# Low parts of weights by adding transfers, and GpSimd's work in another order, in a one-layer decoder step

## The chip, the cores and the metric

The kernel runs on one core of a Trainium2 chip. The metric is the device time of one execution in microseconds. A core has five engines that run beside each other and meet by semaphores: TensorE (PE in the profile, its weight loads PEld), VectorE (DVE), ScalarE (ACT), GpSimd (POOL) and SyncE (SP), which here issues most of the transfers. Each engine takes its instructions in the order in which they were put in its queue.

## What is computed

One inference step of one layer of width 2048, for 256 new tokens of a prompt and 8 x 4 tokens of running sequences (288 columns in all). Cut to what matters:

```python
h = rmsnorm(x, norm1_g)
proj = h @ w_in + b_in                      # 2048 -> 3072
a, gate, z = split(proj, 1024)
u = a * sigmoid(gate)
u_ext = concat([hist_conv, u])              # 30 older rows
c = silu(layernorm(depthwise_causal_conv(u_ext, conv_w, 31 taps) + conv_b))
z_ext = concat([hist_pool, z])              # 15 older rows
d = mean over windows (2, 4, 8, 16) of z_ext, by group of 256 columns, minus z
p = (d @ pool_w, by group) * pool_scale
x = x + concat([c, p]) @ w_out              # 2048 -> 2048
h2 = rmsnorm(x, norm2_g)
x = x + square(relu(h2 @ w_ff1)) @ w_ff2    # 2048 -> 8192 -> 2048
y = rmsnorm(x, norm_f)                      # also returned: the new u and z history
```

## The kernel before

All data lies with channels on the 128 partitions and the 288 tokens along the free dimension. To keep float32 precision, each product of a weight tile and an activation tile is done in three matmuls: high weight by high activation, low weight by high activation, high weight by low activation. For that every weight is split on the chip into a high part (`whi`, rounded by ScalarE) and a low part (`wlo`, the rest).

A weight block is loaded by SyncE in two halves of 512 KB (`load`, line 164), each into one of six raw buffers `wr`. `split` (line 276) makes the two parts of each half, each into one of five buffers, so a high part can be written only when TensorE is done with the part five before. How the low part comes about is set by a letter in `WAYS` (line 73), one for each half in turn:

- V: VectorE subtracts, one instruction of 128 x 1024 (line 265);
- G: GpSimd subtracts, two instructions of 128 x 512 (line 268);
- D: ScalarE writes the negated high part (line 262), and a transfer issued by GpSimd adds the weights to it from memory (line 263). D needs the raw buffer only for the high part.

`SEQUENCE` (line 45) gives the first stages: eight conv blocks c0 to c7, four pool groups p3 to p0 and their small products P3 to P0. A conv block or a pool group is 96 matmuls, and takes two weight blocks, that is four parts; a small product is 12 matmuls and one part of half length. Then follow w_out on the pool half (the projection, weights w0 to w7), w_out on the conv half, and the two feed-forward products in four chunks. In `gemm` (line 296) the matmuls of two k and one output bank come in sixes: two with whi, two with wlo, two with whi. The weights of a stage are split while the stage before is multiplied.

A conv block's result goes through VectorE and ScalarE (`conv_pair`, line 427), then through 31 taps on VectorE (lines 446 to 448); for the running sequences GpSimd multiplies all windows by the taps (`prd`, line 451) and VectorE sums them (line 453). The taps are emitted under `later()`, with a low urgency. The sums of the conv blocks feed a mean (`ln_mean`) inside the sixth product of the projection. A pool group (`pool_group`, line 464) goes through doubling sums on GpSimd (line 479), three small GpSimd operations (lines 483, 486, 487) with a VectorE subtraction between them (line 484), and a split into `dx`; `pool_products` (line 495) multiplies it.

The order of each queue is set when the program is built: a scheduler that simulates the engines picks by urgency and by what is ready in its simulation. `tc.issue_after(x)` puts an instruction behind x in the order of issue. `classes` (line 317) reorders the next matmuls of a `gemm` by the parity of the activation row that they read; `TURN` (line 70) is such an order and stands in c2, c5, the projection's first product, its products g = 5 and g = 7, in g = 2 of the conv half, and in the feed-forward's second product. `between` places other work inside a `gemm`, ahead of the pair (k, bank) named as its key.

Of the kernel before, what the change touches and what calls it, by code (L numbers as in the profile page):

```python
# [12 lines left out]
ALU = mybir.AluOpType  # L13
# [56 lines left out]
TURN = "110100" * 4 + "01" * 6 + "1100" * 3  # L70


WAYS = {"c2": "GVGV", "c3": "GDGG", "c4": "GDGD", "p3": "GDDG", "c5": "GDGD", "c": "GGGV", "p": "GVVG", "w0": "VV", "w": "GG", "ff": "VV"}


VEC = (("norm1_g", 16), ("b_in", 24), ("conv_b", 8), ("ln_g", 8), ("ln_b", 8), ("pool_scale", 8), ("norm2_g", 16), ("norm_f", 16))
# [10 lines left out]
def trunk_kernel(ctx: ExitStack, tc: tile.TileContext, io):  # L87
# [18 lines left out]
    def nm(s):  # L106
        seen[s] = seen.get(s, 0) + 1
        return f"{s}{seen[s]}"
# [25 lines left out]
    def f32(t):  # L134
        return t.bitcast(F32)
# [25 lines left out]

    blocks = iter(range(5, io["w"].shape[0]))

    def load():

        src, raw = io["w"][next(blocks)], []
        for h in range(2):
            raw.append((raw_tile(), src[:, 4 * h : 4 * h + 4, :]))
            nc.sync.dma_start(*raw[-1])
        return raw  # L170
# [81 lines left out]
    turns = {}  # L252

    def split_part(raw, src, hi, lo, way):

        nc.scalar.copy(hi, raw)  # L260
        if way == "D":
            nc.scalar.activation(lo, f32(hi), AF.Copy, scale=-1.0)
            nc.gpsimd.dma_start(lo, src, accum_op=ALU.add)
        elif way == "V":
            nc.vector.tensor_tensor(lo, raw, f32(hi), op=ALU.subtract)  # L265
        else:
            for j in range(0, raw.shape[1], 2):
                nc.gpsimd.tensor_tensor(lo[:, j : j + 2, :], raw[:, j : j + 2, :], f32(hi[:, j : j + 2, :]), op=ALU.subtract)  # L268
# [7 lines left out]
    def split(halves, stage="ff"):  # L276

        parts = []
        for raw, src in halves:
            turns[stage] = turns.get(stage, -1) + 1  # L280
            parts.append(spl())
            ways = WAYS.get(stage) or WAYS[stage[0]]
            split_part(raw, src, *parts[-1], ways[turns[stage] % len(ways)])
        return lambda k, m: columns(*parts[k // 4], k % 4, m)
# [8 lines left out]
            chain[0] = last.ins  # L293
        return last

    def gemm(banks, rhs, m_outer=False, between={}, classes="", by_part=False, gets=None, pairs=None):


        n = len(rhs)
        gets = gets or ready.pop(0)  # L300
        todo, begins = [], {}
        if by_part:
            for k in range(0, n, 2):
                sets = [range(len(banks))] if k else [range(2), range(2, len(banks))]
                for last, ms_ in enumerate(sets, 1 - len(sets)):
                    for part, (w, x) in enumerate(((0, 0), (1, 0), (0, 1))):
                        if last == 0:
                            begins[len(todo)] = (k, None, k + 1)[part]
                        todo += [(k + (1 - d if x else d), m, w, x) for m in ms_ for d in range(2)]
        else:  # L310
            pairs = pairs or [(k, m) for k in range(0, n, 2) for m in range(len(banks))]
            if m_outer:
                pairs.sort(key=lambda km: km[1])
            for k, m in pairs:
                begins[len(todo)] = (k, m) if m else k
                todo += [(k + d, m, w, x) for d, w, x in ((0, 0, 0), (1, 0, 0), (0, 1, 0), (1, 1, 0), (1, 0, 1), (0, 0, 1))]
        head = todo[: len(classes)]
        for j, c in enumerate(classes):
            todo[j] = next(p for p in head if c == "." or (p[0] + p[3]) % 2 == int(c))
            head.remove(todo[j])  # L320
# [91 lines left out]
    rb = row("rb")  # L412


    cs, pcs = [], []
    sum_c = tmpp.tile([P, 2, T], F32, name="sum_c", tag="ag2", bufs=2)

    def history(i):
# [8 lines left out]
    def conv_pair(i, banks):  # L427
# [8 lines left out]
            nc.vector.scalar_tensor_tensor(out=out, in0=a, scalar=v("b_in", i), in1=b, op0=ALU.add, op1=ALU.mult)  # L436
        if i % 2 == 0:
            cs.append(actp.tile([P, 2, T], F32, name=nm("c"), tag="c", bufs=4))
        c = cs[i // 2][:, i % 2, :]
        with later():  # L440
            if i % 2 == 0:
                pcs.append(cvp.tile([P, 2, SEQ], F32, name=nm("pc"), tag="cv"))
            pc = pcs[i // 2][:, i % 2, :]
            cwv = vec[:, CWO + i * CW : CWO + (i + 1) * CW]
            nc.scalar.activation(pc, up[:, 0:SEQ], AF.Identity, bias=v("conv_b", i), scale=cwv[:, 0:1])  # L445
            for w in range(1, CW):
                dst = pc if w < CW - 1 else c[:, 0:SEQ]
# [3 lines left out]
            nc.gpsimd.tensor_tensor(prd[:, :, :, 0:CW], windows(us, CW), cwv[:, None, None, :].to_broadcast([P, NB, NS, CW]), op=ALU.mult)  # L451
# [12 lines left out]
    def pool_group(g):  # L464
# [19 lines left out]
        nc.vector.scalar_tensor_tensor(out=d[:, :, 0:SEQ], in0=s[:, :, PH:ZO], scalar=1.0 / w, in1=z[:, :, PH:ZO], op0=ALU.mult, op1=ALU.subtract)  # L484
        news = [x[:, :, ZO:ZL].rearrange("p m (b t) -> p m b t", t=ZS)[:, :, :, PH:] for x in (s, z)]
        nc.gpsimd.tensor_scalar(news[0], news[0], 1.0 / w, None, op0=ALU.mult)
        nc.gpsimd.tensor_tensor(d[:, :, SEQ:T].rearrange("p m (b t) -> p m b t", t=NS), news[0], news[1], op=ALU.subtract)
        dh, dl = act2("dx", tag="p", bufs=4)
        nc.scalar.copy(dh, d)
        nc.vector.tensor_tensor(dl, d, f32(dh), op=ALU.subtract)  # L490
# [34 lines left out]
    for kind, i in SEQUENCE[3:-1]:  # L525
        if (kind, i) == ("P", 1):
            continue
        if kind == "c":
            conv_pair(i, conv_products(i, classes=TURN if i == 5 else "", **(dict(gets=ahead(1), between={12: lambda: pool_products(1)}) if i == 7 else {})))
# [9 lines left out]
    gemm(each(bks[0]) + each(bks[1]), proj, gets=[lambda k, m: both_gets[m // 2][0](k, m % 2)], between={(0, 2): lambda: pool_products(0)}, classes="." * 36 + TURN, pairs=early + [(6, m) for m in range(4)])  # L539
    chain.clear()  # L540
    load_table(AF.Abs_reciprocal_sqrt, f32(mixp[1][0])[:, 0:1])
    with later(2 * LATER):
# [53 lines left out]
    chain.append(last)  # L596
    bks = [bank2() for _ in range(2)]
    two_gets = [ahead(0) for _ in range(2)]
    gemm(each(bks[0]) + each(bks[1]), mixc, gets=[lambda k, m: two_gets[m // 2][0](k, m % 2)])
    chain.clear()  # L600
    for g in range(8):
        bk = bks[g] if g < 2 else bank2()
# [179 lines left out]
```

## Time and profile before

| | us |
|---|---|
| median of three runs | 1082.34 (1081.94 to 1082.63) |
| the profiled execution | 1082.43 |
| its span, first to last instruction | 1080.6 |

The page's first part gives each engine's busy time; its fourth the chain of work that ended last. In the timeline a row is: start, duration, engine, line, operation, output<-inputs, shape, count, and in brackets the idle time before it with what ended it. In the windows view a row is a stretch of time, its length, then busy time and number of instructions of PE, PEld, DVE, ACT and POOL, the granted TensorE clock, the busy share of the transfer engines and GB/s. The waits view reads: engine, what it was about to write, its line, what it waited for, total us, times, longest.

### The profile page before, as it was taken

What the parts mean: (1) busy time and instruction counts of PE and PEld (TensorE: products, weight loads), DVE (VectorE), ACT (ScalarE), POOL (GpSimd) and SP (SyncE); (2) the same over time, 40 slices, a digit from 0 to 9 for tenths busy, and PEclk for the clock granted to TensorE, in tenths of its full rate; (3) what the DMA queues carried; (4) which work ended last, traced back from release to release, by engine and by line L of the source; (5) the groups of instructions that cost most, each with busy time, mean ns of one, the idle gap of its engine ahead of it and who ended that gap; (6) DMA issues with size and microseconds to landing.
All of it is one profiled execution on the core that took longest, in us unless ns stands there. A gap on an engine that the chain in (4) does not pass through costs nothing.

```text
span 1080.6 us, 19528 instructions
## 1 busy us (share of the span) xinstructions
PE 1069.2 (99%) x8176; PEld 1067.9 (99%) x8176; DVE 633.7 (59%) x810; ACT 479.0 (44%) x588; POOL 175.9 (16%) x182
## 2 busy tenths in 40 slices
PE   9999999999999999999999999999999999999996
PEld 8999999999999999999999999999999999999996
DVE  7899999788654544444554444555544445554553
ACT  8654445665544433334443333444433334444441
POOL 0878979512000000000000000000000000000001
PEclk9999999999999999999999999999999999999999
DMA  9896478555555555555555555555555555555522
GB/s 326 288 263 182 145 187 247 177 171 173 162 173 166 169 175 163 170 173 165 170 174 164 170 170 167 171 173 162 173 168 167 173 171 164 173 166 170 172 79 88
DMA packets 58296, 190.71 MB, mean 176 GB/s; under 512 B 6240, under 2 KB 11232, under 8 KB 58208
## 3 DMA queue, kind: packets, MB, share of 16 engines
q1 hardware_dynamic: 56336, 184.35, 54.3%
q0 software_dynamic: 1008, 3.67, 1.9%
q8 instruction: 64, 1.05, 0.4%
q10 hardware_dynamic: 864, 1.44, 0.4%
q14 instruction: 24, 0.20, 0.0%
HBM read 185.16 MB, written 4.28 MB: 175 GB/s over the span
## 4 chain that ended last, share of the span: by engine, by line
PE 75%; issue 21%; ACT 2%; POOL 1%; DMA 1%; SPq 0%; POOLq 0%; DVE 0%
PE ac L291 74%; POOL wlo L268 1%; DMA wr<-in_w 1%; ACT whi L349 1%; PE pp L291 1%; DMA wlo<-in_w 1%; ACT hx L354 0%; ACT z_all L405 0%; POOL prd L451 0%; POOL xT L718 0%; ACT whi L260 0%; SPq L191 0%; POOLq L768 0%; DVE xT L691 0%; ACT whi L356 0%
## 5 line engine op out<-in xcount | busy, mean ns | idle before, releaser
L260 ACT CAST whi<-wr 128x1024 fp32r<-128x1024 f32 (+1 forms) x332 | 346.5, 1044 | 551.3 <-PE ac L291 536.7
L265 DVE TENSOR_TENSOR wlo<-wr,whi 128x1024 fp32r<-128x1024 f32 x288 | 353.5, 1227 | 348.1 <-ACT whi L260 348.1
L291 PE MATMUL ac<-ax,whi 128*128 128x288 f32 x2048 | 351.0, 292 | 0.0
L291 PE MATMUL ac<-fx,whi 128*128 128x288 f32 x2048 | 350.2, 292 | 0.0
L291 PEld LDWEIGHTS ac<-ax,whi 128*128 128x128 f32 x2048 | 296.0, 187 | 0.0
L291 PEld LDWEIGHTS ac<-fx,whi 128*128 128x128 f32 x2048 | 295.6, 187 | 0.0
L291 PE MATMUL ac<-ax,wlo 128*128 128x288 f32 x1024 | 217.3, 292 | 0.0
L291 PE MATMUL ac<-fx,wlo 128*128 128x288 f32 x1024 | 216.4, 292 | 0.0
L291 PEld LDWEIGHTS ac<-ax,wlo 128*128 128x128 f32 x1024 | 162.5, 187 | 0.0
L291 PEld LDWEIGHTS ac<-fx,wlo 128*128 128x128 f32 x1024 | 162.2, 187 | 0.0
L291 PE MATMUL ac<-hx,whi 128*128 128x288 f32 x768 | 131.9, 296 | 1.4 <-DVE hx L352 1.4
L718 POOL TENSOR_TENSOR xT<-xT,rf 128x288 f32<-128x288 f32 x4 | 3.1, 795 | 799.9 <-ACT rf L722 799.9
L291 PEld LDWEIGHTS ac<-hx,whi 128*128 128x128 f32 x768 | 112.6, 190 | 1.8 <-ACT hx L354 1.7
L268 POOL TENSOR_TENSOR wlo<-wr,whi 128x512 fp32r<-128x512 f32 x74 | 102.4, 1433 | 17.1 <-ACT whi L260 16.0
L448 DVE SCALAR_TENSOR_TENSOR pc<-u_all,vec,pc 128x256 f32<-128x256 f32 x232 | 99.3, 479 | 1.9 <-ACT pc L445 0.7
L291 PE MATMUL ac<-hx,wlo 128*128 128x288 f32 x384 | 80.4, 295 | 0.2 <-DMA wlo<-in_w 0.2
L291 PEld LDWEIGHTS ac<-hx,wlo 128*128 128x128 f32 x384 | 61.1, 189 | 0.4 <-DMA wlo<-in_w 0.4
L291 PE MATMUL ac<-dx,whi 128*128 128x288 f32 x256 | 46.8, 295 | 0.0
L291 PE MATMUL ac<-mx,whi 128*128 128x288 f32 x256 | 44.9, 293 | 0.0
L660 DVE SCALAR_TENSOR_TENSOR t<-ac,r 128x576 f32<-128x576 f32 x32 | 24.2, 757 | 25.4 <-PE ac L291 25.3
L291 PEld LDWEIGHTS ac<-dx,whi 128*128 128x128 f32 x256 | 38.4, 188 | 0.2
L291 PEld LDWEIGHTS ac<-mx,whi 128*128 128x128 f32 x256 | 37.5, 188 | 0.2 <-DVE xT L579 0.2
(129 smaller groups left out, 529.6 us busy)
## 6 DMA issues: line engine op xcount, KB each, us to landing
wr<-in_w SPq DMA_DIRECT2D x335, 512.0 KB, 3.8
wlo<-in_w POOLq DMA_DIRECT2D x7, 512.0 KB, 7.8
xT<-in_xT SPq DMA_DIRECT2D x8, 288.0 KB, 7.7
wr<-in_w SPq DMA_DIRECT2D x5, 256.0 KB, 3.9
out_u_out<-u_all SPq DMA_DIRECT2D x1, 1208.0 KB, 9.6
u_all<-in_hist_c SPq DMA_DIRECT2D x8, 136.0 KB, 5.3
out_z_out<-z_all SPq DMA_DIRECT2D x1, 668.0 KB, 9.2
z_all<-in_hist_p SPq DMA_DIRECT2D x4, 152.0 KB, 6.6
```

What stands on the lines that cost most here:

```text
L260: nc.scalar.copy(hi, raw)
L265: nc.vector.tensor_tensor(lo, raw, f32(hi), op=ALU.subtract)
L268: nc.gpsimd.tensor_tensor(lo[:, j : j + 2, :], raw[:, j : j + 2, :], f32(hi[:, j : j + 2, :]), op=ALU.subtract)
L291: last = nc.tensor.matmul(*args, **kw)
L349: nc.scalar.copy(hi[:, blocks[0]], raw[:, blocks[0]])
L448: nc.vector.scalar_tensor_tensor(out=dst, in0=up[:, w : w + SEQ], scalar=cwv[:, w : w + 1], in1=pc, op0=ALU.mult, op1=ALU.add)
L660: nc.vector.scalar_tensor_tensor(out=t, in0=bk[:, :, :T], scalar=0.0, in1=both(rows2[0]), op0=ALU.max, op1=ALU.mult)
L718: eng.tensor_tensor(xk, xk, r[:, None, :].to_broadcast([P, n, T]), op=ALU.mult)
```

## The change

- `WAYS`: the second low part of each of p2, p1, p0 and the third (V) become D, and the second of c6 and of c7 (G) become D: eight in all. The second of c4 goes from D to G, the first of w0 from V to G. There were seven D parts, there are fourteen.
- `prd` of conv blocks 0 and 1 is issued behind the first adding transfer, that of block 2 behind the second, those of all later blocks behind the third. The taps of blocks 2 and 3 are emitted one block later.
- GpSimd's weight subtractions of c7 and w0 are issued behind p1's last GpSimd operation, those from w1 on behind p0's. In a pool group VectorE's subtraction now stands behind the three small GpSimd operations.
- P1's products stand 24 matmuls earlier in c7 (k = 8 instead of 12), P0's 12 matmuls earlier in the projection.
- The halves of w0 to w7 are loaded in the other order, the half used first being loaded first. The first 24 matmuls of the projection take all high weights before the low ones (`late`).
- The first product of the conv half takes, for its first four k, two banks to the end before the other two (`mixed`).

```diff
-WAYS = {"c2": "GVGV", "c3": "GDGG", "c4": "GDGD", "p3": "GDDG", "c5": "GDGD", "c": "GGGV", "p": "GVVG", "w0": "VV", "w": "GG", "ff": "VV"}
+WAYS = {"c2": "GVGV", "c3": "GDGG", "c4": "GGGD", "p3": "GDDG", "c5": "GDGD", "c": "GDGV", "p": "GDDG", "w0": "GV", "w": "GG", "ff": "VV"}
...
-    def load():
+    def load(order=(0, 1)):
...
-        for h in range(2):
+        for h in order:
...
-            nc.gpsimd.dma_start(lo, src, accum_op=ALU.add)
+            added.append(nc.gpsimd.dma_start(lo, src, accum_op=ALU.add))
...
-                nc.gpsimd.tensor_tensor(lo[:, j : j + 2, :], ...)
+                with tc.issue_after(pooled[-1].ins) if pooled else nullcontext():
+                    nc.gpsimd.tensor_tensor(lo[:, j : j + 2, :], ...)
...
+        todo[:late] = sorted(todo[:late], key=lambda p: p[2])
...
-            get = split(load(), f"w{j}")
-            yield [lambda k, m, get=get: get(korder[k], m)]
+            get = split(load((1, 0)), f"w{j}")
+            yield [lambda k, m, get=get: get(korder[k] ^ 4, m)]
...
+        while waiting:
+            taps(*waiting.pop())
+        if i in (2, 3):
+            waiting.append((i, up, us))
+        else:
+            taps(i, up, us)
+
+    def taps(i, up, us):
...
-            nc.gpsimd.tensor_tensor(prd[:, :, :, 0:CW], ...)
+            with tc.issue_after(added[max(0, min(2, i - 1))].ins):
+                nc.gpsimd.tensor_tensor(prd[:, :, :, 0:CW], ...)
...
-        nc.vector.scalar_tensor_tensor(out=d[:, :, 0:SEQ], ...)
...
-        nc.gpsimd.tensor_tensor(d[:, :, SEQ:T]..., news[0], news[1], op=ALU.subtract)
+        last = nc.gpsimd.tensor_tensor(d[:, :, SEQ:T]..., news[0], news[1], op=ALU.subtract)
+        newest[g] = last
+        nc.vector.scalar_tensor_tensor(out=d[:, :, 0:SEQ], ...)
...
+        if i == 7:
+            pooled.append(newest[1])
...
-... between={12: lambda: pool_products(1)} ...
+... between={8: lambda: pool_products(1)} ...
...
+    pooled.append(newest[0])
...
+    mixed = [(k, m) for k in range(0, KT // 2, 2) for m in range(4)]
+    mixed.sort(key=lambda km: (km[0] // 4, km[1] // 2) if km[0] < 4 else (1, 0))
-    gemm(..., between={(0, 2): lambda: pool_products(0)}, classes="." * 36 + TURN, ...)
+    gemm(..., late=24, between={4: lambda: pool_products(0)}, classes="." * 24 + TURN, ...)
...
-    gemm(each(bks[0]) + each(bks[1]), mixc, gets=[...])
+    gemm(each(bks[0]) + each(bks[1]), mixc, gets=[...], pairs=mixed)
```

More of the change, by code (lines that the diff above doesn't have):

```diff
@@ L70 @@
 TURN = "110100" * 4 + "01" * 6 + "1100" * 3
-WAYS = {"c2": "GVGV", "c3": "GDGG", "c4": "GDGD", "p3": "GDDG", "c5": "GDGD", "c": "GGGV", "p": "GVVG", "w0": "VV", "w": "GG", "ff": "VV"}
+WAYS = {"c2": "GVGV", "c3": "GDGG", "c4": "GGGD", "c5": "GDGD", "c": "GDGV", "p": "GDDG", "w0": "GV", "w": "GG", "ff": "VV"}
 VEC = (("norm1_g", 16), ("b_in", 24), ("conv_b", 8), ("ln_g", 8), ("ln_b", 8), ("pool_scale", 8), ("norm2_g", 16), ("norm_f", 16))
@@ L250, in row_of_sums @@
         return row_of(psum, psum[:, 0, :T], *args), last
-    turns = {}
+    turns, added, newest, pooled = {}, [], {}, []
     def split_part(raw, src, hi, lo, way):
@@ L267, in split_part @@
             for j in range(0, raw.shape[1], 2):
-                nc.gpsimd.tensor_tensor(lo[:, j : j + 2, :], raw[:, j : j + 2, :], f32(hi[:, j : j + 2, :]), op=ALU.subtract)
+                with tc.issue_after(pooled[-1].ins) if pooled else nullcontext():
+                    nc.gpsimd.tensor_tensor(lo[:, j : j + 2, :], raw[:, j : j + 2, :], f32(hi[:, j : j + 2, :]), op=ALU.subtract)
     def spl():
@@ L294, in mm, with gemm @@
         return last
-    def gemm(banks, rhs, m_outer=False, between={}, classes="", by_part=False, gets=None, pairs=None):
+    def gemm(banks, rhs, m_outer=False, between={}, classes="", by_part=False, gets=None, pairs=None, late=0):
         n = len(rhs)
@@ L412, in trunk_kernel @@
     rb = row("rb")
-    cs, pcs = [], []
+    cs, pcs, waiting = [], [], []
     sum_c = tmpp.tile([P, 2, T], F32, name="sum_c", tag="ag2", bufs=2)
@@ L450, in conv_pair @@
             nc.scalar.activation(prd[:, :, :, CW], ones[:, 0 : NB * NS].rearrange("p (b t) -> p b t", t=NS), AF.Identity, bias=v("conv_b", i), scale=0.0)
-            nc.gpsimd.tensor_tensor(prd[:, :, :, 0:CW], windows(us, CW), cwv[:, None, None, :].to_broadcast([P, NB, NS, CW]), op=ALU.mult)
+            with tc.issue_after(added[max(0, min(2, i - 1))].ins):
+                nc.gpsimd.tensor_tensor(prd[:, :, :, 0:CW], windows(us, CW), cwv[:, None, None, :].to_broadcast([P, NB, NS, CW]), op=ALU.mult)
             cso = c[:, SEQ:T]
@@ L483, in pool_group @@
         nc.gpsimd.tensor_tensor(first_sums, first_sums, rcnt[:, None, w - 2 : 2 * w - 3].to_broadcast([P, 2, w - 1]), op=ALU.mult)
-        nc.vector.scalar_tensor_tensor(out=d[:, :, 0:SEQ], in0=s[:, :, PH:ZO], scalar=1.0 / w, in1=z[:, :, PH:ZO], op0=ALU.mult, op1=ALU.subtract)
         news = [x[:, :, ZO:ZL].rearrange("p m (b t) -> p m b t", t=ZS)[:, :, :, PH:] for x in (s, z)]
         nc.gpsimd.tensor_scalar(news[0], news[0], 1.0 / w, None, op0=ALU.mult)
-        nc.gpsimd.tensor_tensor(d[:, :, SEQ:T].rearrange("p m (b t) -> p m b t", t=NS), news[0], news[1], op=ALU.subtract)
+        last = nc.gpsimd.tensor_tensor(d[:, :, SEQ:T].rearrange("p m (b t) -> p m b t", t=NS), news[0], news[1], op=ALU.subtract)
+        newest[g] = last
+        nc.vector.scalar_tensor_tensor(out=d[:, :, 0:SEQ], in0=s[:, :, PH:ZO], scalar=1.0 / w, in1=z[:, :, PH:ZO], op0=ALU.mult, op1=ALU.subtract)
         dh, dl = act2("dx", tag="p", bufs=4)
@@ L527, in trunk_kernel @@
             continue
+        if i == 7:
+            pooled.append(newest[1])
         if kind == "c":
-            conv_pair(i, conv_products(i, classes=TURN if i == 5 else "", **(dict(gets=ahead(1), between={12: lambda: pool_products(1)}) if i == 7 else {})))
+            conv_pair(i, conv_products(i, classes=TURN if i == 5 else "", **(dict(gets=ahead(1), between={8: lambda: pool_products(1)}) if i == 7 else {})))
         elif kind == "p":
@@ L538, in trunk_kernel @@
     early.sort(key=lambda km: km[1] // 2)
-    gemm(each(bks[0]) + each(bks[1]), proj, gets=[lambda k, m: both_gets[m // 2][0](k, m % 2)], between={(0, 2): lambda: pool_products(0)}, classes="." * 36 + TURN, pairs=early + [(6, m) for m in range(4)])
+    mixed = [(k, m) for k in range(0, KT // 2, 2) for m in range(4)]
+    mixed.sort(key=lambda km: (km[0] // 4, km[1] // 2) if km[0] < 4 else (1, 0))
+    gemm(each(bks[0]) + each(bks[1]), proj, gets=[lambda k, m: both_gets[m // 2][0](k, m % 2)], late=24, between={4: lambda: pool_products(0)}, classes="." * 24 + TURN, pairs=early + [(6, m) for m in range(4)])
     chain.clear()
@@ L598, in trunk_kernel @@
     two_gets = [ahead(0) for _ in range(2)]
-    gemm(each(bks[0]) + each(bks[1]), mixc, gets=[lambda k, m: two_gets[m // 2][0](k, m % 2)])
+    gemm(each(bks[0]) + each(bks[1]), mixc, gets=[lambda k, m: two_gets[m // 2][0](k, m % 2)], pairs=mixed)
     chain.clear()
```

## The prediction

> **What bounds the kernel now.** I read the page first, then the waits of the weight loads, then single stretches of TensorE.
>
> ```profile
> span 1080.6 us, 19528 instructions
> PE 1069.2 (99%) x8176; PEld 1067.9 (99%) x8176; DVE 633.7 (59%) x810; ACT 479.0 (44%) x588; POOL 175.9 (16%) x182
> PEld ac L291 <- DMA wlo<-in_w: 0.4, 1, 0.4
> PEld ac L291 <- DVE xT L579: 0.2, 1, 0.2
> ```
>
> TensorE is the bound: 99% of the span, and the change leaves its number of matmuls alone. Only time in which TensorE waits or runs slower than it can is to be won. In the part of the program that the diff touches the waits view names two such places: one wait for an adding transfer (0.4 us), one for a VectorE addition that empties an accumulator (0.2 us).
>
> The timeline shows that each costs more than its wait. The products come in sixes (four with whi, two with wlo), so the start of one wlo pair to the next is six matmuls:
>
> ```profile
> 49.29 0.42 PE L291 MATMUL ac<-hx,wlo 128*128 128x288 f32 x2
> ...
> 50.42 0.54 PE L291 MATMUL ac<-hx,wlo 128*128 128x288 f32 x2 [0.20 <-DMA wlo<-in_w]
> ...
> 51.32 0.43 PE L291 MATMUL ac<-hx,wlo 128*128 128x288 f32 x2
> ...
> 72.12 0.43 PE L291 MATMUL ac<-hx,wlo 128*128 128x288 f32 x2
> ...
> 72.92 0.43 PE L291 MATMUL ac<-hx,wlo 128*128 128x288 f32 x2
> ...
> 144.30 0.42 PE L291 MATMUL ac<-hx,wlo 128*128 128x288 f32 x2
> ...
> 145.08 0.42 PE L291 MATMUL ac<-hx,wlo 128*128 128x288 f32 x2
> ...
> 218.93 0.42 PE L291 MATMUL ac<-mx,wlo 128*128 128x288 f32 x2
> ...
> 219.93 0.30 PE L291 MATMUL ac<-mx,wlo 128*128 128x288 f32 x1
> ```
>
> Undisturbed, a six takes 0.78 us (144.30 to 145.08; 130 ns a matmul). The pair due at 49.29 + 0.78 = 50.07 starts at 50.42, the next at 51.32 instead of 51.20: 0.35 + 0.12 = **0.47 us** lost on the spot. Long after that a six takes 0.80 us (72.12 to 72.92). TensorE has fallen into a slower cadence, and it stays there:
>
> ```profile
> 53.00:85.00 32.00, 32.00 (x242) 32.00 (x241) 29.47 (x71) 18.44 (x22) 24.28 (x20) 1.00 0.96 258
> 98.00:130.00 32.00, 32.00 (x248) 32.00 (x247) 30.49 (x61) 15.80 (x24) 30.21 (x28) 1.00 0.47 147
> ```
>
> In 32 us it does 242 matmuls there and 248 later, at the same granted clock, 1.00. Between lies the order TURN in c5 (line 529); I take it that TURN ends the slow cadence, as the counts on both sides of it say.
>
> What made the transfer late is in the chain of work:
>
> ```profile
> 40.16 0.20 POOL prd L451
> ...
> 42.27 2.14 POOL prd L451
> 44.41 5.97 DMA wlo<-in_w
> ...
> 50.42 60.24 PE ac L291 x454
> 39.26 1.06 ACT L262 ACTIVATE wlo<-whi 128x1024 fp32r<-128x1024 f32 x1
> ```
>
> The negated copy was there at 39.26 + 1.06 = 40.32, but GpSimd did two history products (prd, conv blocks 0 and 1) first and issued the transfer at 44.41; it landed at 50.38.
>
> **The change part by part.**
>
> *prd behind the transfers.* The first adding transfer can be issued at 40.32, 4.1 us earlier.
>
> ```profile
> L265 DVE TENSOR_TENSOR wlo<-wr,whi 128x1024 fp32r<-128x1024 f32 x284 | 350.2, 1233 | 348.1 <-ACT whi L260 348.1
> L268 POOL TENSOR_TENSOR wlo<-wr,whi 128x512 fp32r<-128x512 f32 x74 | 102.4, 1433 | 17.1 <-ACT whi L260 16.0 <-issue 1.0
> L262 ACT ACTIVATE wlo<-whi 128x1024 fp32r<-128x1024 f32 x7 | 7.4, 1059 | 0.2
> L263 POOL DMA_DIRECT2D wlo<-in_w x7 | 6.5, 927 | 4.5 <-ACT wlo L262 3.3 <-issue 1.0
> DMA to landing us min/median/max: 6.0/7.8/10.2
> ```
>
> The seven transfers took 6.0 to 10.2 us from issue to landing, this one 6.0. So it lands at 46.3, at the median at 48.1; both beat 50.07. The maximum (50.5) would not; I take the near end, as it is the same transfer. That removes 0.47 us and the slow cadence behind it: 70 matmuls left in c3 plus 96 each in c4 and p3 are 262, or 44 sixes at 0.02 us, 0.87 us. **Gain 1.34 us.** The moved prd instructions feed only the conv sums; these end 195.26 + 0.46 against a matmul at 197.96, 2.2 us spare:
>
> ```profile
> 195.26 0.46 DVE L553 TENSOR_TENSOR sum_c<-pmean,c 128x288 f32<-128x288 f32 x1
> 197.96 0.65 PE L291 MATMUL pmean<-sum_c,ones 128*128 128x288 f32 x2
> ```
>
> and VectorE gets lighter, so holding back the taps of blocks 2 and 3 costs nothing. Without that cover, what the sums lose beyond 2.2 us stalls TensorE.
>
> *Order `mixed`.* At the end of the second wait the pair due at 219.71 starts at 219.93: 0.22 us; 84 of that block's 96 matmuls follow, 14 sixes at 0.02 = 0.28 us, until TURN in g = 2. With `mixed` the accumulator in question is needed 12 matmuls (1.56 us) later than now, and the wait was 0.2 us. The price is that the second pair of mx is needed 12 matmuls earlier, its low rows at 219.97; VectorE had written them at 218.84 (218.09 + 0.75):
>
> ```profile
> 218.09 0.75 DVE L590 TENSOR_TENSOR mx<-n,mx 128x576 fp32r<-128x576 f32 x1
> ```
>
> **Gain 0.50 us.**
>
> *Eight more D parts, c4.1 from D to G, w0.0 from V to G.* Counts: VectorE loses seven low parts, 8.6 us; ScalarE gains seven copies, 7.4 us; GpSimd loses two parts and gains two (four instructions each way) and gains seven issues, +6.5 us; 3.6 MB more are moved. Neither engine limits TensorE there, so nothing is gained on the path. What counts is lateness. A part's cast waits for the buffer of five parts before, so each part has a fixed lead. The shortest lead of a new D part is that of c7's second part: cast at 145.06, first wlo matmul at 154.44.
>
> ```profile
> 145.06 1.05 ACT L260 CAST whi<-wr 128x1024 fp32r<-128x1024 f32 x1 [1.43 <-issue]
> ...
> 154.44 0.42 PE L291 MATMUL ac<-hx,wlo 128*128 128x288 f32 x2
> ```
>
> 145.06 + 1.05 + 1.06 = 147.17, plus 6.0, 7.8 or 10.2 is 153.2, 155.0 or 157.4: 1.3 early, 0.5 late, 2.9 late. The 6.0 us were those of the first transfer, with no other adding transfer beside it; this one has the nearest other one 11 us ahead of it, and the transfers' share of time in 98 to 130 us is 0.47 against 0.96 in 53 to 85 us, where most of the seven ran. So I take 6.0 and no stall, and keep both ends. The other new parts have leads longer by 1.5 us or more, by the same count.
>
> [...]
>
> *GpSimd behind the pool groups, P1 at k = 8.*
>
> ```profile
> 157.56 0.42 PE L291 MATMUL ac<-hx,wlo 128*128 128x288 f32 x2
> 159.03 0.75 DVE L490 TENSOR_TENSOR dx<-d,dx 128x576 fp32r<-128x576 f32 x1
> 145.50 5.05 POOL L268 TENSOR_TENSOR wlo<-wr,whi 128x512 fp32r<-128x512 f32 x4
> ...
> 150.67 2.54 POOL L268 TENSOR_TENSOR wlo<-wr,whi 128x512 fp32r<-128x512 f32 x2
> ```
>
> P1's products come 24 matmuls earlier, at 157.30 by the old clock (the start of the six whose wlo pair starts at 157.56); their input was done only at 159.78. Alone that would stall 2.5 us. But 5.05 + 2.54 us of weight subtractions between the group's sums now queue behind its last operation, so the input comes some 7 us earlier. Behind the new queue order waits c7's first G part: the sums end at 145.5, three small operations and 2.5 us of subtraction follow, about 149, for a use at 151.32 (four sixes before 154.44). Cost nothing.
>
> *Halves of w_out, late, P0 at 4.* The same loads and matmuls in another order. The half used first is now loaded first and its low parts are asked for 16 matmuls (2.1 us) in, which is cover for the move of that part to GpSimd. P0 comes 12 matmuls earlier:
>
> ```profile
> 165.42 0.74 DVE L490 TENSOR_TENSOR dx<-d,dx 128x576 fp32r<-128x576 f32 x1
> ```
>
> That is after 24 matmuls of the stage, at about 168.2; its input was done at 166.16. Nothing gained, nothing lost.
>
> **Sum**: the profiled execution took 1082.43 us (1.8 outside its span), the median shown is 1082.34. 1082.43 - 1.34 - 0.50 = 1080.59; from the median 1080.5. I write **1080.6 us**, 0.16% less.
>
> **The rivals.**
>
> *One D part a little late.* c7's second part with the median 7.8 us: 0.5 late, 0.12 for the restart, then the slow cadence to the TURN of the projection (82 matmuls of c7 and 36 more, to about 169.8: 19 sixes, 0.39): about **1081.6**. For it: p3's transfers took up to 10.2; against: traffic. With 10.2 it is 1084.0.
>
> *A D part behind the pool sums: slower.* p2's second part, until now VectorE's, becomes a transfer issued by GpSimd just when that does p3's sums:
>
> ```profile
> 88.82 1.06 ACT L260 CAST whi<-wr 128x1024 fp32r<-128x1024 f32 x1 [0.88 <-PE ac L291]
> 89.36 2.71 POOL L479 TENSOR_TENSOR s<-z_all 128x422 f32<-128x422 f32 x2
> 92.03 6.55 POOL L479 TENSOR_TENSOR s<-s 128x420 f32<-128x420 f32 x6
> 101.40 0.42 PE L291 MATMUL ac<-hx,wlo 128*128 128x288 f32 x2
> ```
>
> It could go at 88.82 + 1.06 + 1.06 = 90.9. Put behind all eight sums it goes at 98.6, lands at 104.6 and is needed at 101.40: 3.2 us late, 0.1 restart, and the slow cadence from there to 169.8 (85 sixes, 1.7 us). 1080.6 + 5.0 = **1085.6**, slower. The stall begins when the issue is later than 95.4; the sum passes +0.2% when it is later than 97.5. For it: a weight part of GpSimd that was ready then also went only at 98.55. Against: at 145.50 the weight parts went ahead of the sums.
>
> *The change does not do what it says*: the first transfer is late all the same (another instruction ahead of it, or traffic). Only 0.50 is won: **1081.9**.
>
> [...]
>
> **How the numbers follow.** Forecast 0.52, with a further 0.08 for somewhat more (other short slow stretches gone too); one part late 0.20; not what it says 0.05; descriptors 0.03; behind the sums 0.12. This kernel's measurement can tell about 0.2% (2.2 us) from no change. Below 1080.2 lies the 0.08: faster 0.08; slower 0.12 (the sums); the same 0.80. The range reaches from 1079.9 (forecast less the spread of the runs and the remains) to 1084.0 (a part with the longest transfer) and leaves out most of the slower case.
>
> **What would show it.** Right: no wait of the weight loads for wlo<-in_w near 50; the transfer issued near 40.4; sixes of 0.78 us through c3, c4 and p3 and through the mx block; 248 matmuls in any 32 us from 53. Wrong: a wait for wlo<-in_w between 90 and 160, with sixes of 0.80 behind it; an issue of L263 after 97 for p2; a wait of the pp matmuls for dx.

## The result, and the profile after

| | before | after |
|---|---|---|
| median, us | 1082.49 (1081.94 to 1082.75, 4 runs) | 1095.80 (1093.99 to 1098.82, 4 runs) |
| ratio, 95% interval | 1 | 1.0126 [1.0100, 1.0153] |
| the profiled execution, span, us | 1082.43, 1080.6 | 1094.48, 1092.7 |

Slower by 1.26%, where 0.16% faster was forecast. (In the diff quoted ahead the new `WAYS` has a key p3; the kernel has none, and p3 takes the letters of p, the same four.)

The page's first lines, of the changed kernel:

```profile
span 1092.7 us, 19547 instructions
...
PE 1071.2 (98%) x8176; PEld 1068.6 (98%) x8176; DVE 632.2 (58%) x803; ACT 486.0 (44%) x595; POOL 177.0 (16%) x189
```

and its waits view (what TensorE was about to write, what it waited for, total us, times, longest):

```profile
PE pp L292 <- ACT dx L502: 3.9, 1, 3.9
PE ac L292 <- DMA wlo<-in_w: 2.6, 2, 2.4
PE pp L292 <- DVE dx L503: 2.4, 1, 2.4
```

The small products (pp) wait twice for their input dx, which they did not before, and conv blocks wait 2.6 us for adding transfers (0.2 us before). To see where the 12.1 us of span went, I took the start of every matmul, and for each stage the sum of what the intervals between starts have over the undisturbed 130 ns. In us, for this kernel and three of the experiments below:

| stage | before | after | p3's operations first | letters put back | VectorE relieved |
|---|---|---|---|---|---|
| c3, c4, p3 | 1.33 | 0.00 | 0.00 | 0.00 | 1.16 |
| p2, P3 | 0.00 | 8.17 | 0.00 | 0.00 | 0.00 |
| c6, p1, P2 | 0.00 | 1.32 | 2.82 | 0.00 | 0.00 |
| p0 | 0.00 | 0.80 | 1.67 | 0.00 | 0.00 |
| c7 with P1 | 0.00 | 3.00 | 2.61 | 0.00 | 0.00 |
| next 400 matmuls (projection) | 0.79 | 0.90 | 0.90 | 5.86 | 1.39 |
| the 400 behind them (start of the mixed stage) | 0.58 | 0.10 | 0.09 | 0.10 | 0.09 |

These stages account for 11.6 of the 12.1 us. The rest lies ahead of c3, where the same sum goes from 1.37 to 2.52 us over the traces of all runs here, so it says nothing of the change.

The two gains that the prediction counted are there: 1.33 us in c3 to p3 and 0.48 us in the mixed stage. The other stages of the table lose, P3 most of all. GpSimd's timeline around P3's input, of the kernel before:

```profile
92.03 6.55 POOL L479 TENSOR_TENSOR s<-s 128x420 f32<-128x420 f32 x6
98.55 2.99 POOL L268 TENSOR_TENSOR wlo<-wr,whi 128x512 fp32r<-128x512 f32 x2
101.50 0.25 POOL L483 TENSOR_TENSOR s<-s,rcnt 128x30 f32<-128x30 f32 x1
102.56 0.39 POOL L486 TENSOR_SCALAR s<-s 128x64 f32<-128x64 f32 x1 [0.81 <-DVE d L484]
103.03 2.54 POOL L268 TENSOR_TENSOR wlo<-wr,whi 128x512 fp32r<-128x512 f32 x2
105.54 0.33 POOL L487 TENSOR_TENSOR d<-s,z_all 128x64 f32<-128x64 f32 x1
```

and of the changed kernel:

```profile
90.69 0.83 POOL L263 DMA_DIRECT2D wlo<-in_w  x1
91.29 1.14 POOL L491 TENSOR_TENSOR s<-s 128x420 f32<-128x420 f32 x1
93.23 0.87 POOL L263 DMA_DIRECT2D wlo<-in_w  x1 [0.80 <-ACT wlo L262]
93.84 2.01 POOL L491 TENSOR_TENSOR s<-s 128x416 f32<-128x416 f32 x2
95.52 2.81 POOL L269 TENSOR_TENSOR wlo<-wr,whi 128x512 fp32r<-128x512 f32 x2
98.01 2.36 POOL L491 TENSOR_TENSOR s<-s 128x408 f32<-128x408 f32 x2
102.86 2.55 POOL L269 TENSOR_TENSOR wlo<-wr,whi 128x512 fp32r<-128x512 f32 x2 [2.49 <-ACT whi L260]
105.37 2.21 POOL L463 TENSOR_TENSOR prd<-u_all,vec 128x992 f32<-128x992 f32 x1
107.53 0.27 POOL L495 TENSOR_TENSOR s<-s,rcnt 128x30 f32<-128x30 f32 x1
107.86 0.39 POOL L497 TENSOR_SCALAR s<-s 128x64 f32<-128x64 f32 x1
108.31 0.90 POOL L263 DMA_DIRECT2D wlo<-in_w  x1
108.96 0.61 POOL L498 TENSOR_TENSOR d<-s,z_all 128x64 f32<-128x64 f32 x1
```

p3's sums end at 100.37 in the changed kernel (98.01 + 2.36). Its three small operations (0.27, 0.39 and 0.61 us in these rows) could follow. But ahead of them in the queue stand the subtraction of c6's first part, for whose cast GpSimd idles 2.49 us, and a product of 2.21 us; a transfer stands between the second and the third. So the last of them ends at 109.57 instead of some 101.6 (an estimate: 100.37 and the three durations). With transfers among the sums the scheduler placed the three operations later (the run with the letters alone, below, shows that they suffice for it), and GpSimd kept that order even while it idled. VectorE and ScalarE then need from 109.94 to 113.3 for the high part of dx, with P3 wanted at 109.31; 2.62 us of that is VectorE's subtraction, which took 0.69 us in the kernel before. The windows view (busy time and count of PE, PEld, DVE, ACT, POOL; then the granted clock) shows a second loss:

```profile
110.00:123.00 13.00, 7.19 (x37) 6.84 (x38) 12.54 (x22) 4.76 (x10) 10.15 (x11) 0.74 0.41 100
```

TensorE's matmuls have a gap of 4.2 us there, up to 113.38, and a second one of 2.9 us, up to 116.95. Behind both they start 240 ns apart instead of 130, the last of them at 120.24; the mean granted clock of this stretch is 0.74. I call this half clock: from 113.6 to 120.5 alone the mean granted clock is 0.51. From 116.95 it took 3.5 us until the starts were 130 ns apart again.

The late adding transfer is c7's second part. The timeline, rows of GpSimd and of TensorE:

```profile
153.75 0.33 POOL L498 TENSOR_TENSOR d<-s,z_all 128x64 f32<-128x64 f32 x1
154.04 3.00 POOL L269 TENSOR_TENSOR wlo<-wr,whi 128x512 fp32r<-128x512 f32 x2
156.99 0.89 POOL L263 DMA_DIRECT2D wlo<-in_w  x1
...
163.09 0.69 PE L292 MATMUL ac<-hx,whi 128*128 128x288 f32 x4
166.18 0.53 PE L292 MATMUL ac<-hx,wlo 128*128 128x288 f32 x2 [2.39 <-DMA wlo<-in_w]
```

and its row in the DMA view from 156 to 167 us (KB, us from issue to landing):

```profile
wlo<-in_w POOLq DMA_DIRECT2D x1, 512.0 KB, 9.1
```

It is issued behind c7's first subtraction, which the change itself had put behind p1's last operation, and lands 9.1 us later. ScalarE's copy for it was done at 156.10, so the queue cost it 0.9 us, and the transfer's own time is the larger part.

### The profile page after: what moved, and what is told of

The parts are those of the page before. It is cut to its first block, busy times and chain, and to the rows that moved or that the text cites. A ratio compares the mean times of both kernels' runs of the same rounds, so it can differ in the third digit from the quotient of the medians.

```text
span 1092.7 us, 19547 instructions
## 1 busy us (share of the span) xinstructions
PE 1071.2 (98%) x8176; PEld 1068.6 (98%) x8176; DVE 632.2 (58%) x803; ACT 486.0 (44%) x595; POOL 177.0 (16%) x189
## 4 chain that ended last, share of the span: by engine, by line
PE 74%; issue 20%; DVE 2%; DMA 1%; POOL 1%; ACT 1%; SPq 0%; POOLq 0%; DVEq 0%; ACTq 0%
PE ac L292 73%; DMA wlo<-in_w 1%; DVE pc L459 1%; DMA wr<-in_w 1%; PE pp L292 1%; POOL wlo L269 0%; POOL s L491 0%; DVE wlo L265 0%; DVE d L500 0%; POOL xT L736 0%; ACT hx L356 0%; ACT whi L351 0%; DVE z_all L409 0%; ACT z_all L407 0%; DVE wlo L360 0%
## 5 line engine op out<-in xcount | busy, mean ns | idle before, releaser
L265 DVE TENSOR_TENSOR wlo<-wr,whi 128x1024 fp32r<-128x1024 f32 (+1 forms) x281 | 346.4, 1233 | 348.1 <-ACT whi L260 348.1
L269 POOL TENSOR_TENSOR wlo<-wr,whi 128x512 fp32r<-128x512 f32 x74 | 98.9, 1404 | 22.9 <-ACT whi L260 21.5
```

## The experiments

Three theories stood at first. **Q**: the order of GpSimd's queue, as read above. **V**: VectorE's subtraction, moved behind the small operations, makes dx late. **D**: the new adding transfers come late for themselves. Each run is told with its ratio to the kernel before, on the same chip (1081.95 to 1082.23 us on these chips).

### The eight letters alone, in the kernel before

```diff
-"c": "GGGV", "p": "GVVG"
+"c": "GDGV", "p": "GDDG"
```

> The kernel before with the eight new D parts alone (the letters for p and c, nothing else). Theory Q (queue): laid into GpSimd's queue, the transfers move p3's three small operations behind c6's first weight subtraction and the prd of block 5, so P3 waits for its input. It expects a wait of the pp matmuls for dx of 4 us or more near 109 to 116, matmuls at half speed behind it, and 1090 to 1097 us. Theory V (VectorE's subtraction put behind the small operations is what makes the input late): no wait of pp, at most a late D part, 1082 to 1084 us.

Measured: 1093.93 us, ratio 1.0104 [1.0090, 1.0118]. Waits view:

```profile
PE pp L291 <- ACT dx L489: 5.6, 1, 5.6
PE ac L291 <- DMA wlo<-in_w: 1.5, 3, 0.7
```

The letters alone bring P3's wait (5.6 us), a lower granted clock (mean of a run 0.992 to 0.995, in the kernel before 0.995 to 0.998), and late transfers (1.5 us in three waits). VectorE's subtraction is not moved here, so V isn't needed for that wait.

### VectorE's subtraction alone

```diff
-        nc.vector.scalar_tensor_tensor(out=d[:, :, 0:SEQ], ...)
         news = ...
...
+        nc.vector.scalar_tensor_tensor(out=d[:, :, 0:SEQ], ...)
```

> The kernel before with VectorE's subtraction in the pool groups put behind the three small GpSimd operations, nothing else. Theory Q: the small operations stay where they were in GpSimd's queue, no wait, 1082.5 us within 0.5. Theory V: a wait of the pp matmuls for dx of about 4 us, 1088 to 1094 us.

Measured: 1083.49 us, ratio 1.0012 [1.0003, 1.0021]. No product pp waits; TensorE waits 0.6 us for one of p3's transfers and 0.7 us at the projection for a low part by VectorE. V falls as the cause of P3's wait.

### p3's operations first

The changed kernel, with GpSimd's subtractions from c6 on and the product of block 5 put behind p3's last operation; all fourteen transfers stay.

```diff
+        if (kind, i) == ("P", 3):
+            pooled.append(newest[3])
...
-            with tc.issue_after(added[max(0, min(2, i - 1))].ins):
+            with tc.issue_after(added[max(0, min(2, i - 1))].ins if i != 5 else newest[3].ins):
```

> The changed kernel, with the weight subtractions from c6 on and the prd of block 5 issued behind p3's last small operation; all fourteen D parts stay. Theory Q: P3's wait (4.1 + 2.7 us), the half speed behind it (about 1.5 us) and the slow cadence go, the late D part of c7 (2.6 us) stays: 1084 to 1088 us, unless p2's small operations now come late in the same way. Theory V: P3 waits as before, 1094 us or more.

Measured: 1088.50 us, ratio 1.0061 [1.0046, 1.0076]. The timeline, rows of GpSimd and of TensorE:

```profile
97.24 2.35 POOL L491 TENSOR_TENSOR s<-s 128x408 f32<-128x408 f32 x2
99.67 0.59 POOL L495 TENSOR_TENSOR s<-s,rcnt 128x30 f32<-128x30 f32 x1
100.33 0.39 POOL L497 TENSOR_SCALAR s<-s 128x64 f32<-128x64 f32 x1
100.80 0.33 POOL L498 TENSOR_TENSOR d<-s,z_all 128x64 f32<-128x64 f32 x1
...
108.55 0.42 PE L292 MATMUL pp<-dx,whi 128*128 128x288 f32 x2
```

and the wait that is left, in the waits view:

```profile
PE ac L292 <- DMA wlo<-in_w: 4.7, 4, 2.0
```

The small operations follow the sums, and P3 waits for nothing. So 7.3 us of the 13.3 (1095.8 less 1088.5) are the queue's order, Q. The rest is what theory D says: four transfers late, one each in c6, p1, p0 and c7. The transfers issued from 90 us on took 7.4 to 9.6 us to land, median 9.3.

### The products and the mixed order alone, in the kernel before

The products and taps behind the transfers, c4 GGGD, and `mixed`: all that the prediction gave a gain to, and nothing else.

```diff
+            with tc.issue_after(added[max(0, min(2, i - 1))].ins):
...
-"c4": "GDGD"
+"c4": "GGGD"
...
+... mixc, gets=[...], pairs=mixed)
```

> The kernel before with two parts of the change alone: prd and the taps behind the adding transfers (with c4's second part by GpSimd), and the order mixed. By the prediction's terms both waits of before and the slow cadence behind them go: 1.34 + 0.50 us, 1080.6 us. If the cadence isn't tied to the waits: 0.7 us, 1081.8 us.

Measured: 1083.78 us, ratio 1.0015 [1.0006, 1.0024], where my sum gave 1080.6. c3 and c4 show no excess and the mixed stage's wait is gone, as forecast. But TensorE waits 0.6 us for p3's transfers, P1 waits 0.8 us for dx, and the projection waits for VectorE (dx, 0.9 us). Something takes the gain back further on.

### The changed kernel without its eight transfers

```diff
-"c": "GDGV", "p": "GDDG"
+"p3": "GDDG", "c": "GGGV", "p": "GVVG"
```

> The changed kernel with the letters of c6, c7 and of p2, p1, p0 as before (GGGV, GVVG): the eight new adding transfers are taken out, every other edit stays. GpSimd's queue then holds the three small operations of p3 right behind its sums again. Theory Q+D (the loss is the order of GpSimd's queue around p3's small operations, which the transfers between the sums brought about, plus late adding transfers of c6 to c7): all of it goes, no wait of P3 for dx, no wait for wlo at c6 to c7, 1080.6 to 1082.3. Rival (the other edits have a cost of their own, as the pair of edits moved behind the transfers had in the kernel before with 1083.8): 1083.5 to 1085, with the loss from p3's adding transfers or from the projection.

Measured: 1086.04 us, ratio 1.0037 [1.0024, 1.0050]; the rival is right. From c3 up to the projection this kernel has no excess in the table, and reaches it 1.31 us ahead of the kernel before (163.79 against 165.10), which is the first gain to 0.03 us. There it loses all of it and 3.8 us more. The timeline's rows of TensorE:

```profile
168.82 0.53 PE L292 MATMUL pp<-dx,whi 128*128 128x288 f32 x2 [1.75 <-DVE dx L515]
...
173.84 0.37 PE L292 MATMUL ac<-dx,whi 128*128 128x288 f32 x1 [1.59 <-DVE u_all L438]
```

and the windows view:

```profile
136.00:149.00 13.00, 13.00 (x102) 13.00 (x102) 13.00 (x25) 7.33 (x12) 10.54 (x12) 1.00 0.50 161
149.00:162.00 13.00, 13.00 (x102) 13.00 (x102) 13.00 (x26) 5.76 (x10) 11.71 (x11) 1.00 0.56 141
162.00:175.00 13.00, 9.66 (x72) 9.23 (x72) 12.93 (x28) 6.14 (x8) 11.40 (x9) 1.00 0.96 281
```

VectorE (the third busy time) has next to no idle time from 136 to 175 us, and TensorE stands still for it. It was as full in the kernel before: 13.00 of 13 us in both of the first two windows. Theory **VE**: the end of this stage is VectorE's, so what TensorE gains ahead of it is waited off.

That explains the 1.31 us. For the 3.8 us more, VectorE's list must also end later: P0's dx was done at 166.16 before and is done at 167.94 here. In part the change makes this itself. Before, GpSimd waited for VectorE's subtraction in each pool group; now that subtraction stands behind the small operations, and so beside GpSimd's weight subtractions. VectorE's subtraction for P0, in the kernel before, and then both of VectorE's operations for P0 here (the second took 0.74 us before):

```profile
161.62 0.68 DVE L484 SCALAR_TENSOR_TENSOR d<-s,z_all 128x512 f32<-128x512 f32 x1
```

```profile
161.73 1.33 DVE L500 SCALAR_TENSOR_TENSOR d<-s,z_all 128x512 f32<-128x512 f32 x1
166.49 1.45 DVE L503 TENSOR_TENSOR dx<-d,dx 128x576 fp32r<-128x576 f32 x1
```

In all the traces of this case together, the first operation took 0.68 to 0.69 us when GpSimd computed nothing meanwhile (15 times), and up to 2.63 us beside GpSimd's work. No run changes this alone, so its share of the 3.8 us isn't measured.

### VectorE relieved

```diff
-"p": "GVVG"
+"p": "GAAG"
...
+        elif way == "A":
+            nc.scalar.activation(lo, f32(hi), AF.Copy, scale=-1.0)
```

> As the run with the letters of c6 to p0 put back (1086.0), but VectorE is relieved of its two 128x1024 subtractions (1.2 to 1.7 us each) in each of p2, p1 and p0; ScalarE writes the negated high part there as for an adding transfer, and the adding itself is left out, so the low parts of these six lack the weight and nothing loads GpSimd or the DMA engines for them. Theory VE (VectorE, busy 13.00 of 13 us from 136 to 162 us, holds P0's input and the projection's banks, and spends again what TensorE gained before): the waits of 2.0, 1.9 and 0.7 us at the projection go to under 0.5 us together and the time to 1080.5 to 1081.7, which is what I had forecast for the whole change. Rival G (the waits come from GpSimd's order around P0 or from P0's earlier place): at least 2 us of wait stay, 1083.5 to 1086.

Measured: 1081.05 us, ratio 0.9987 [0.9978, 0.9995]; 5.0 us below the run that it is made from. The windows view:

```profile
149.00:162.00 13.00, 13.00 (x102) 13.00 (x102) 13.00 (x24) 6.08 (x10) 11.24 (x11) 1.00 0.89 188
162.00:175.00 13.00, 13.00 (x101) 13.00 (x101) 11.53 (x26) 8.70 (x12) 11.36 (x10) 1.00 0.90 273
```

TensorE has 101 matmuls in the last window instead of 72, and VectorE idles. The projection's excess is 1.39 us instead of 5.86. VE stands: to take six of the seven subtractions off VectorE, as the change does, brings 4.5 us at the projection, more than twice the 1.84 us that I had counted as the whole gain. (Way A leaves out the addition of the weights, so these six low parts are not what the layer needs; the run gives a time only.)

### P0 back in its place

The same without the transfers, and the projection as in the kernel before.

```diff
-... late=24, between={4: lambda: pool_products(0)}, classes="." * 24 + TURN
+... between={(0, 2): lambda: pool_products(0)}, classes="." * 36 + TURN
...
-            get = split(load((1, 0)), f"w{j}")
+            get = split(load(), f"w{j}")
```

> As the run with the letters of c6 to p0 put back (1086.0), and P0's place, the order of the projection's halves and its first 24 matmuls as in the kernel before. Theory VE (VectorE ends that stage when it ends, whatever TensorE gained): P0 is wanted 1.6 us later, so 1.5 to 3 us of the 4.6 us of waits go, 1083 to 1084.5, not below the kernel before. Rival (the earlier place of P0 alone made the loss): all waits go, 1080.6 to 1081.5.

Measured: 1085.94 us, ratio 1.0031 [1.0019, 1.0043]. My size was wrong: the time doesn't move. The waits only sit elsewhere, on a low part by VectorE (2.0 us) and on dx (0.8 us), with half clock behind the first (mean granted clock 0.87 from 162 to 175 us). VectorE begins to write P0's dx at 166.40 here and at 166.49 in the run with P0 at 4. That is VE in a purer form than I had it: the place where TensorE asks made no difference here, VectorE's list did.

### Part of the eight transfers

First only the six of p2, p1 and p0, with p3's operations first (`"c": "GGGV"`).

> As the run with p3's small operations first (1088.5), and the letters of c6 and c7 back to GGGV: six of the eight new transfers stay, those of p2, p1 and p0. Theory D (single late transfers cost what TensorE waits for them): the 1.2 and 2.2 us of c6 and c7 go, the 0.7 and 1.3 us of p1 and p0 stay, 1084 to 1085.5. Rival (the waits come from GpSimd's longer order, whoever uses it): c7 still waits for its second part by 1 us or more, 1086 to 1088.5.

Measured: 1086.91 us, ratio 1.0043 [1.0029, 1.0057]; neither theory as it stood. The time lies in the rival's range, but c7 waits for nothing, as D says. Instead p1's first transfer, for which TensorE waited 0.5 us in the run with p3's operations first, now makes it wait 2.0 us, with half clock behind that (mean granted clock 0.79 from 126 to 134 us). GpSimd's order had changed again with the letters.

Then p2's two alone, with p3's operations first and P0 back in its place (`"p2": "GDDG", "c": "GGGV", "p": "GVVG"`).

> As the run with P0 back in place, but p2's two subtractions on VectorE become adding transfers again, with p3's small operations first on GpSimd. These two are the only ones of the eight new transfers that made no wait in any run so far; they relieve VectorE by 2 x 1.2 us. Theory VE: waits at the projection fall by about 2.4 us against the run with P0 back, 1080.6 to 1082. Rival: p2's transfers or p3's come late by their 9 us, or the relief at 100 us is used up before the projection: 1083 or more.

Measured: 1086.49 us, ratio 1.0033 [1.0021, 1.0046]. The time is the rival's, for another reason. p2's transfers make no wait, and the relief of VectorE does reach P0's dx: VectorE begins it at 164.12, where it was 166.40 with P0 back and none of the eight transfers. But in this program's order VectorE makes a low part of the projection behind that dx, from 166.00 on instead of 164.88, and TensorE waits 1.6 us for it, with half clock behind that (mean granted clock 0.87 from 162 to 175 us).

### The mixed order alone, in the kernel before

> The kernel before with the edit of the mixed stage's order alone. The step of the prediction (the gap of 0.5 us at the start of the mixed stage goes, nothing else changes): 0.5 us less, 1081.6 to 1081.9, ratio 0.9995. Rival (the saving is taken up by the stage behind it): no change, ratio 1.000.

Measured: 1081.88 us, ratio 0.9995 [0.9986, 1.0003]. The trace has no wait in the mixed stage and nothing new. This is the lowest time of the kernels that compute the whole layer; it can't be told from the kernel before.

### Why a transfer takes 9 us

Two kernels made from the one without the eight transfers (1086.0). There GpSimd issues c4's transfer at 59.08 with block 2's product right behind it, and the first packet starts 4.34 us after the issue (starts of packets are from the trace's records), where lone transfers in the kernel before needed 1.7 to 1.9. First the product goes to VectorE, so that nothing stands right behind:

> As the run with the letters of c6 to p0 put back, and block 2's multiply of the new tokens (L463, 2.48 us on GpSimd) goes to VectorE, so that nothing stands right behind the second adding transfer of c4 on GpSimd until the subtractions of p3's first part. Theory S (GpSimd's next instruction holds up the packets of an adding transfer): first packet 1.6 to 2.2 us after the issue of that transfer instead of 4.1, landing 6 to 7 us after it; p3's two transfers are issued 2 us earlier. Theory L (its packets stand behind the loads that SyncE issued shortly before): first packet still 3.5 to 4.3 us after issue. Time by either 0 to 0.5 us below the run without this edit, more only if p3's transfers are late there.

Measured: the first packet 3.89 us after the issue. S falls. (The time, 1091.78 us, ratio 1.0092 [1.0076, 1.0107], is another matter: VectorE took 8.97 us for the product, and p3's transfers came 5 us late.) Then the product is put ahead of the transfer:

> As the run with the letters of c6 to p0 put back, but block 2's multiply (2.2 to 2.5 us on GpSimd) stands ahead of c4's adding transfer instead of right behind it, so that the transfer is issued some 2.2 us later (61.3 instead of 59.08) behind the same loads, the newest of them issued at 58.83. Theory L (its packets stand behind those loads, whose first landing was at 63.73): first packet at 63.3 to 63.9 as before, so only 2.0 to 2.6 us after the issue instead of 4.34, and landing near 67.6 as before, 6 to 7 us after the issue instead of 8.48. Theory F (a transfer takes what it takes, whenever it is issued): first packet 4.3 us after the issue, landing near 69.8. The time stays within 1 us of the run it is made from (1086.0), which VectorE sets at the projection.

Measured: 1085.82 us, ratio 1.0037 [1.0023, 1.0052]. The transfer was issued 1.55 us later and landed 0.93 us earlier (66.63 against 67.56). GpSimd's timeline without the edit and with it:

```profile
59.08 0.88 POOL L263 DMA_DIRECT2D wlo<-in_w  x1 [0.28 <-POOL wlo L269]
59.69 2.47 POOL L463 TENSOR_TENSOR prd<-u_all,vec 128x992 f32<-128x992 f32 x1
```

```profile
58.49 2.42 POOL L464 TENSOR_TENSOR prd<-u_all,vec 128x992 f32<-128x992 f32 x1
60.63 1.11 POOL L264 DMA_DIRECT2D wlo<-in_w  x1
```

and the view of the low parts from 58.5 to 64.5 us, in which this is the one transfer, again without and with it:

```profile
DMA to landing us min/median/max: 8.5/8.5/8.5
```

```profile
DMA to landing us min/median/max: 6.0/6.0/6.0
```

The first packet started at 62.47, the instant at which the newest load ahead of it (issued at 58.77) began to land. Without the edit that load began to land at 63.73 and the packet started at 63.42. So L's own numbers (63.3 to 63.9) missed, since the load itself came earlier, but the packet came with the load, and F falls. The load was also complete at 63.82 instead of 67.28, so where the two were issued side by side, both were slower.

L fits elsewhere too. I take the transfers of all traces that were issued when the adding transfer before them had landed. With a load issued less than a microsecond ahead, the first packet came 2.0 to 4.5 us after the issue, in all 24 cases within 0.4 us of that load's first landing. With a load issued up to 0.4 us behind it, it came after 2.9 to 4.3 us; these are five, and c7's second part is one. The other 21 needed 1.6 to 2.3 us. That the delay goes with the load and not with the issue is shown by the one shift above; the rest is agreement, and what holds both isn't shown.

## Why the prediction was wrong

The steps that failed are two that the sum put at nothing: GpSimd's new order ("Cost nothing") and the lateness of the new transfers ("no stall"). The first was worth 7.3 us of the 13.3, by the run that undoes it; late transfers made most of the rest. The two gains, 1.84 us, were right and far too small to matter.

- **prd behind the transfers, 1.34 us.** Right in place and size: issue at 41.07 (I had 40.32), no wait, 248 matmuls from 53 to 85 us, 1.33 us gone. It landed at 49.25, after 8.2 us instead of the 6.0 that I took, still in time. But that the moved products and taps cost nothing else is doubtful: with them and `mixed` alone, P1 and the projection waited 1.7 us for their dx. Which edit did it wasn't tried.
- **Order `mixed`, 0.50 us.** Right: 0.48 us in the trace; alone it gave 0.3 us of median, which the measurement can't tell from nothing.
- **"Neither engine limits TensorE there, so nothing is gained on the path."** Wrong, though the 13.3 us don't come from it: the changed kernel reaches the projection 12.1 us late (177.20 against 165.10) and loses hardly more there than the kernel before (0.90 against 0.79). My own row had VectorE busy for 30.49 of 32 us in 98 to 130 us, and the sum made nothing of it. From 136 us on VectorE was full (13.00 of 13 us in each of two windows up to 162, 12.96 in the next, in the kernel before), and P0 and the projection hang on it. So a gain of TensorE ahead of that point isn't kept (1.31 us ahead, then 5.9 lost, without the transfers), and the relief of VectorE, which I put at nothing, was worth 4.5 us there. That the relieved kernel then takes 1081.05 us, near the forecast of 1080.6, is luck: in its trace p3's stage loses 1.16 us again, and of the 1.1 us by which its span is shorter than that of the kernel before, 1.0 lies ahead of c3 (which begins at 45.65 instead of 46.69).
- **Lateness of the new parts: c7's second, 6.0 us, no stall.** Wrong in issue and size. I let it go at its copy's end; it went 0.9 us later, behind the first subtraction of c7, which the edit `pooled` had put behind p1. And it took 9.1 us, with the median of the eight new ones at 9.0. Sparse traffic, my reason for 6.0, wasn't the point: a load was issued 0.08 us behind it. The rival "one D part a little late" had a late transfer at this place, and its upper price, 2.9 us late, is near the 3.0 us of this stage, but partly by luck: the queue's 0.9 us, which it didn't have, and the transfer's 9.1 add up to the 10.2 that it took. It also counted one part, and with p3's operations first there were four.
- **GpSimd behind the pool groups, "cost nothing".** Right for P1, which waited for nothing. Wrong as a whole: I worked out what stood behind the new order for p1 and never for p3. The rival "a D part behind the pool sums" looked at the same stretch of the queue, and had it turned round: the transfers went between the sums, and what came late was the small operations behind them. That is 7.3 us by the run that puts them first, about 1.7 us of it half clock (16 matmuls by 0.11 us). VectorE's subtraction for P3, 2.62 us instead of 0.69, lies in this stretch too.
- **Halves of w_out, late, P0 at 4: nothing.** Right as measured: with P0 back in its place the time was the same (1085.94 against 1086.04).
- **"Descriptors", chance 0.03**: the case that VectorE's work holds up the adding transfers. No run shows such a hold-up or a length for it: in the changed kernel the first packet of the transfer issued at 108.31 came 1.6 us after the issue beside a VectorE at work without a break, and the long delays (up to 4.5 us) go with loads.

Left open: how much of the loss at the projection comes from VectorE's operations being longer beside GpSimd's, and how much from their order. No run was made in which all fourteen transfers are in time, so whether the eight could pay isn't shown.

## What to carry to other kernels

An engine that is off the path by its share of the span was the bound of one stage here (VectorE: 59% of the span before, 13.00 of 13 us from 136 to 149 and again to 162): read its busy time in windows, and where it is full, price every edit there by what it gives to or takes from that engine. When instructions are added to a queue with a static order, read the new order around every short operation that feeds the path; one that is 0.3 to 0.6 us long came 8 us late here behind a neighbour that waited. Look also at what the moved operation will run beside. A transfer's time wasn't its own here: with a load issued less than a microsecond ahead of it, or just behind it, its first packet came up to 4.5 us after the issue, against 1.6 to 2.3.

## What the hardware showed beside this

- Half clock came after shorter gaps as well: 2.3 us between two matmul starts in p1 (the run with six transfers; 240 ns a matmul until 133.4), 2.3 us in the projection (P0 back in place, beginning 1.2 us behind the gap), and gaps of 0.8 and 1.9 us with two matmuls between them (p2's two alone), but not after 2.7 us in the changed kernel's c7 (mean granted clock 1.00 from 163 to 170 us) and 2.3 us in c7 of the run with p3's operations first (1.00 from 155 to 163 us). So the length of a gap alone did not decide it in these runs.
- Some of VectorE's operations were longer beside GpSimd's work, by all the traces of this case: a weight subtraction of 128 x 1024 took 1.20 to 1.23 us in all 3787 cases in which GpSimd computed nothing meanwhile, and over 10% longer in 70 of 232 others, up to 2.32 us. A tap of the convolution (128 x 256) took 0.46 to 0.49 us either way.
- The product of 992 elements that GpSimd does in 2.2 to 2.8 us took VectorE 8.97 us, with GpSimd at work for nearly all of that time; which of the two made it so wasn't tried:

```profile
50.57 8.97 DVE L463 TENSOR_TENSOR prd<-u_all,vec 128x992 f32<-128x992 f32 x1
```
